# Using a streamed adaLN tile one step after its load, in a two-layer hybrid decoder trunk

## The chip, the cores and the metric

The kernel runs on one core of a Trainium2 chip. The metric is the device time of one execution in microseconds (us). Before the change the median of three runs is 1044.76 us (1042.81 to 1046.88).

The core has five engines that run side by side, each through its own list of instructions in a fixed order: TensorE (PE in the profile, its weight loads PEld), VectorE (DVE), ScalarE (ACT), GpSimd (POOL) and SyncE (SP). SyncE here only issues transfers (DMAs) between device memory and on-chip memory. An engine whose next instruction is not ready waits, and everything behind that instruction in its list waits too.

## What is computed

Two layers of a decoder trunk on 256 tokens of width 1024, in float32. In each layer a modulated LayerNorm is followed by one wide input projection, whose columns feed four token mixers (A: differential attention, B: a gated delta rule, C: latent attention, D: dilated attention over three groups), their gates z and the merge gates; then come the branch projections, an output projection and a second LayerNorm.

```python
c_act = jax.nn.silu(c)
for l in range(DEPTH):
    shift, scale, gate = jnp.split(c_act @ w_ada[l] + b_ada[l], 3, axis=-1)
    h = _layernorm(x) * (1.0 + scale[:, None, :]) + shift[:, None, :]
    y = _mixer_sublayer(h, positions, l, w_in[l], ...)
    x = _layernorm(DEEPNORM_ALPHA * x + gate[:, None, :] * y) * ln_g[l] + ln_b[l]
```

The change concerns `c_act @ w_ada[l]`, a vector of 1024 times a matrix of 1024x3072. Its result is needed at the start of a layer (shift, scale) and at its end (gate).

## The kernel before

**Weights.** Nearly all of TensorE's work multiplies the tokens by streamed weights. `load_w` loads a piece of 128x1024 floats (512 KB) into one of the `W_RAW = 4` buffers of the pool `wraw` (tile `wr`, L552); `split` (L486 to L489) then writes it as two halves: ScalarE casts the high part (`wh`, L488), VectorE subtracts it from the piece for the low part (`wl`, L489). TensorE does three matmuls for each product: `token_mm` (L598 to L600, names d, dv, m, br) and `feat_proj` (L635 to L637, names z, b). Pieces of an item are asked for `AHEAD = 2` items before the item is computed. A buffer is free again when its `wl` is written, and SyncE's queue issues the loads in a fixed order: a load whose buffer is not free holds all that stand behind it.

**The rest of adaLN.** The first modulation is loaded at the start into other buffers (L348). Everything else of it, the first layer's gate and the whole of the second layer's, is done by `ada_steps` (L360 to L370) beside the projections, in eight groups of four tiles: groups 4 and 5 of the first layer and 0 to 3 of the second during the first layer, groups 4 and 5 of the second during that layer. A tile `wada` (128x2x512, 512 KB, DMA at L364) takes a buffer of the same pool `wraw`. Its two halves are multiplied by one column of `c_act` each and added up in the tile `ada` by VectorE (`add_ada`: L312 for the first, L313 for the others). When the four tiles of a group are through, `end_ada` sums over the partitions on TensorE (`adac`, L328, or `adag`) and VectorE adds a bias (`modc`, L318, or `gateb`, L337). In the kernel before, the load and its two VectorE instructions are written in the same step.

**Streams.** `ada_steps` and the mixers are generators: each `yield` ends a step, and `step_streams` is called in the middle of a token item and after every item. A stream with rate 0.7, as ada has, gets seven steps in ten calls. So parts of the mixers are written between the matmuls of the projections: the rotary part of D's queries and keys on VectorE (`rope`, L452 to L455, into `tkd`), their transposes on TensorE (`tu_d`, L653, put off by one item through `deferred`), and the triangular inverse of B, which goes through device memory: 16 writes `scr` (L1021), four loads `g_T` and `g_U` (L1026, L1027), then products `px`, `py`, `pu`, `pw` on TensorE with copies on ScalarE (L1039, L1052) and predicated copies into `g_U` on VectorE (L1045).

**Order on each engine.** A scheduler orders each engine's list from the program and a model of durations; `in_order` adds an edge that only fixes the order of two instructions. On the chip the lists are fixed.

Of the kernel before, what the change touches and what calls it, by code (L numbers as in the profile page):

```python
# [202 lines left out]
def kernel(ctx: ExitStack, tc: tile.TileContext, d, out, dbg=None, nlayers=DEPTH):  # L203
# [18 lines left out]
    def slab(which, shape, name):  # L222
        free = int(np.prod(shape[1:]))
        assert free <= 512, (name, shape)
        t = slabs[which].tile([P, 512], F32, tag="slab", name=name)[:shape[0], 0:free]
        if len(shape) == 3:
            t = t.rearrange("p (a b) -> p a b", b=shape[2])
        elif len(shape) == 4:
            t = t.rearrange("p (a b c) -> p a b c", b=shape[2], c=shape[3])
        return t  # L230
# [40 lines left out]
    marks = {}  # L271
# [36 lines left out]
    def add_ada(acc, w, k):  # L308

        cd = cact[:, k:k + 1]  # L310
        if k == 0:
            return V.tensor_scalar(acc, w, cd, None, ALU.mult)  # L312
        return V.scalar_tensor_tensor(acc, w, cd, acc, ALU.mult, ALU.add)  # L313
# [8 lines left out]
    def end_ada(l, g, acc, tag):  # L322
        if g < 4:
            pc = bank(tag, [P, 2, 2], f"adac{l}{g}")
            terms = [(w, cact[:, k:k + 1]) for w, k in direct] + [(acc, ones[:, 0:1])]
            direct.clear()
            marks[f"sum{l}{g}"] = [
                T.matmul(pc[:, i // 2, i % 2:i % 2 + 1], a[:, i * P:(i + 1) * P], b, start=(n == 0 and i == 0),  # L328
                         stop=(n == len(terms) - 1), skip_group_check=True)
                for n, (a, b) in enumerate(terms) for i in range(4)]  # L330
            modulation(l, g, pc)
        else:
            gb = slab("b", [P, 512], f"gateb{l}{g}")
            nc.sync.dma_start(gb, d["bgate"][l:l + 1, (g - 4) * 512:(g - 3) * 512].to_broadcast([P, 512]))
            pb = bank(tag, [P, 512], f"adag{l}{g}")
            T.matmul(pb, ones, acc, start=True, stop=True)
            V.tensor_tensor(gb, pb, gb, ALU.add)  # L337
            gateb[l] = (gateb[l] or []) + [gb]
# [18 lines left out]

    first_slabs = ["p"] * 8 + ["o"] * 6 + ["c"] * 4 + ["tk"] * 4 + ["q"] * 6 + ["d"] * 4

    def ada_steps(l, g):  # L360
        acc = slab("b", [P, 512], f"ada{l}{g}")
        for kk in range(4):
            w = wraw.tile([P, 2, 512], F32, tag="wr", name=f"wada{l}{g}{kk}")
            nc.sync.dma_start(w, d["wada"][l, g, kk])  # L364
            for k in range(2):
                add_ada(acc, w[:, k, :], 2 * kk + k)
            if kk < 3:
                yield
        end_ada(l, g, acc, "sc")
        yield  # L370


    al = cpool.tile([P, DEPTH, 2], F32, name="al")
# [83 lines left out]
    def in_order(*insts):  # L457

        flat = []
        for i in insts:  # L460
            flat += i if isinstance(i, (list, tuple)) else [i]
        for a, b in zip(flat, flat[1:]):
            tc.add_manual_dep(getattr(b, "ins", b), getattr(a, "ins", a).name, mybir.DependencyInfo(mybir.DependencyClass.NoSync, mybir.DependencyReason.SCHED_ONLY),
                              reason="order of issue")
# [22 lines left out]
    def split(hi, lo, src):  # L487
        marks["hi"] = A.copy(hi, src)  # L488
        return [V.tensor_tensor(lo, src, hi.bitcast(F32), ALU.subtract)]  # L489
# [58 lines left out]
    def load_w(src, name, place=None):  # L548

        n = src.shape[-1]  # L550
        w = wraw.tile([P, 1024], F32, tag="wr", name=f"wr{name}")
        nc.sync.dma_start(w[:, 0:n], src)  # L552
        if place is None:
            width = 1024
            hi = [whp.tile([P, 1024], F32R, tag="wh", name=f"wh{name}")]
            lo = [wlp.tile([P, 1024], F32R, tag="wl", name=f"wl{name}")]
        else:
            width = n // 2
            hi = [slab(place(), [P, 512], f"wh{name}_{j}").bitcast(F32R) for j in range(2)]
            lo = [slab(place(), [P, 512], f"wl{name}_{j}").bitcast(F32R) for j in range(2)]  # L560
        marks[f"lo{name}"], marks[f"hi{name}"] = [], []
        for j, (a, b) in enumerate(zip(hi, lo)):
            m = min(n, width)
            marks[f"lo{name}"] += split(a[:, 0:m], b[:, 0:m], w[:, j * width:j * width + m])
            marks[f"hi{name}"].append(marks["hi"])

        def get(c0, m):
            return tuple(a[c0 // width][:, c0 % width:c0 % width + m] for a in (hi, lo))

        return get  # L570
# [137 lines left out]
    def layer_items(l, prev):  # L708
# [752 lines left out]
        def load_out(_):  # L1461
            place = spare()
            L.wo = [load_w(d["wout"][l, 1, p], f"o{p}_{l}", place) for p in range(4)]

        def start_ada(_):
            def steps():
                for l_, g in [(l, 4), (l, 5)] + [(l + 1, g) for g in range(4) if l + 1 < nlayers]:
                    yield from ada_steps(l_, g)
            L.sada = start("ada", steps())
# [136 lines left out]
```

## Time and profile before

| | us |
|---|---|
| median of 3 runs | 1044.76 |
| lowest, highest | 1042.81, 1046.88 |
| profiled execution | 1044.96 |
| its span | 1043.1 |
| TensorE busy | 1021.5 (98% of the span) |
| VectorE busy | 721.7 (69%) |
| ScalarE busy | 541.6 (52%) |
| DMA, share of 16 engines over the span | 53% |

The profiled execution is 1.86 us longer than its span, which is what lies around the first and the last instruction. TensorE's matmuls overlap, so the start of one to the start of the next is what one costs, and its row's duration is longer than that. The clock that was granted to TensorE is 0.992 of full speed over the span; PEclk in a window is 1.00 at full speed (2.4 GHz) and 0.50 at half (1.2 GHz). "Idle before" names the time that an engine had nothing running before an instruction, and the releaser is what ended it.

### The profile page before, as it was taken

The page shows a single profiled execution, that of the slowest core. Times are in us where ns is not written, and L with a number is a line of the kernel's source. Part 1 is how long each engine was busy: PE and PEld are TensorE (multiplying, and loading weights), DVE is VectorE, ACT ScalarE, POOL GpSimd, SP SyncE. Part 2 cuts the span into 40 slices and gives each one's busy share as a digit, 9 for nine tenths or more (in the row PEclk, how much of TensorE's full clock was granted, in tenths as well). Part 3 has the DMA queues.
Part 4 walks back from the last instruction along what each step waited for, and adds up shares of the span by engine and source line. Part 5 has one row for each costly group of instructions (what it writes and reads, how often), then busy time and mean ns, then how long its engine had stood idle before and what let it go on. Part 6 is the DMA issues. An engine that isn't in the chain of part 4 may idle for free.

```text
span 1043.1 us, 16218 instructions
## 1 busy us (share of the span) xinstructions
PE 1021.5 (98%) x5982; PEld 845.1 (81%) x5982; DVE 721.7 (69%) x1583; ACT 541.6 (52%) x1012; POOL 29.4 (3%) x38
## 2 busy tenths in 40 slices
PE   8999999999999979999999999999999999999996
PEld 4599887888887868888866988888889788888885
DVE  4788778885677646666686887788746565566676
ACT  2376675654554535555436656665445454555550
POOL 0000000010000000000000000001000000000000
PEclk8999999999999989999999999999999999999999
DMA  9964344757654576445726334465564255544541
GB/s 331 349 242 141 109 143 160 212 188 239 212 162 159 196 240 210 141 152 184 275 91 209 115 122 142 132 212 175 169 226 145 82 204 172 170 160 143 164 179 41
DMA packets 67406, 185.18 MB, mean 178 GB/s; under 512 B 13696, under 2 KB 17152, under 8 KB 67328
## 3 DMA queue, kind: packets, MB, share of 16 engines
q1 hardware_dynamic: 67328, 184.16, 53.0%
q8 instruction: 47, 0.77, 0.3%
q14 instruction: 31, 0.25, 0.1%
HBM read 179.67 MB, written 4.46 MB: 177 GB/s over the span
## 4 chain that ended last, share of the span: by engine, by line
PE 84%; DMA 8%; DVE 4%; ACT 2%; SPq 1%; issue 1%; DVEq 0%; ACTq 0%
PE m L598 6%; PE m L600 6%; PE m L599 6%; PE d L599 5%; PE d L598 5%; PE d L600 5%; DMA wada<-in_wada 4%; PE z L635 3%; PE z L637 3%; PE z L636 3%; PE br L598 3%; PE br L599 3%; PE br L600 3%; PE first L606 2%; PE b L635 2%; PE b L636 2%
## 5 line engine op out<-in xcount | busy, mean ns | idle before, releaser
L489 DVE TENSOR_TENSOR wl<-wr,wh 128x1024 fp32r<-128x1024 f32 x248 | 302.5, 1222 | 176.7 <-ACT wh L488 174.6
L488 ACT CAST wh<-wr 128x1024 fp32r<-128x1024 f32 x248 | 259.8, 1050 | 234.0 <-issue 50.2
L598 PE MATMUL m<-wh,hh 128*128 128x512 f32 x256 | 102.7, 402 | 0.0
L598 PE MATMUL d<-wh,hh 128*128 128x512 f32 x256 | 102.7, 402 | 0.0
L600 PE MATMUL d<-wh,hl 128*128 128x512 f32 x256 | 102.0, 400 | 0.0
L599 PE MATMUL d<-wl,hh 128*128 128x512 f32 x256 | 101.8, 398 | 0.0
L600 PE MATMUL m<-wh,hl 128*128 128x512 f32 x256 | 101.1, 395 | 0.0
L599 PE MATMUL m<-wl,hh 128*128 128x512 f32 x256 | 100.8, 394 | 0.0
L635 PE MATMUL z<-hh,wh 128*128 128x256 f32 x256 | 74.0, 289 | 0.0
L637 PE MATMUL z<-hh,wl 128*128 128x256 f32 x256 | 73.5, 287 | 0.0
L313 DVE SCALAR_TENSOR_TENSOR ada<-wada,cact,ada 128x512 f32<-128x512 f32 x80 | 59.7, 746 | 19.6 <-DMA wada<-in_wada 18.6
L636 PE MATMUL z<-hl,wh 128*128 128x256 f32 x256 | 73.1, 286 | 0.0
L599 PEld LDWEIGHTS d<-wl,hh 128*128 128x128 f32 x256 | 49.0, 191 | 10.6 <-issue 1.3
L600 PEld LDWEIGHTS d<-wh,hl 128*128 128x128 f32 x256 | 48.9, 191 | 10.4 <-issue 0.7
L635 PE MATMUL b<-hh,wh 128*128 128x256 f32 x192 | 56.3, 293 | 1.0 <-ACT qkva L659 1.0
L598 PEld LDWEIGHTS d<-wh,hh 128*128 128x128 f32 x256 | 49.0, 191 | 9.8 <-issue 0.5
L598 PEld LDWEIGHTS m<-wh,hh 128*128 128x128 f32 x256 | 48.1, 188 | 10.5 <-issue 0.5
L600 PEld LDWEIGHTS m<-wh,hl 128*128 128x128 f32 x256 | 48.1, 188 | 10.5 <-issue 0.5
L599 PEld LDWEIGHTS m<-wl,hh 128*128 128x128 f32 x256 | 48.2, 188 | 9.6 <-issue 0.5
L636 PE MATMUL b<-hl,wh 128*128 128x256 f32 x192 | 55.0, 286 | 0.0
L637 PE MATMUL b<-hh,wl 128*128 128x256 f32 x192 | 54.9, 286 | 0.0
L598 PE MATMUL br<-wh,bh 128*128 128x512 f32 x128 | 51.4, 401 | 0.0
(358 smaller groups left out, 2132.0 us busy)
## 6 DMA issues: line engine op xcount, KB each, us to landing
wr<-in_win SPq DMA_DIRECT2D x208, 512.0 KB
wr<-in_wbr SPq DMA_DIRECT2D x32, 512.0 KB
wada<-in_wada SPq DMA_DIRECT2D x32, 512.0 KB
wada<-in_wada SPq DMA_DIRECT2D x32, 256.0 KB
wro<-in_wout SPq DMA_DIRECT2D x8, 512.0 KB
wr<-in_wout SPq DMA_DIRECT2D x8, 512.0 KB
wrs<-in_win SPq DMA_DIRECT2D x8, 256.0 KB
wrearly<-in_win SPq DMA_DIRECT2D x8, 256.0 KB
```

The source lines that it names most:

```text
L313: return V.scalar_tensor_tensor(acc, w, cd, acc, ALU.mult, ALU.add)
L488: marks["hi"] = A.copy(hi, src)
L489: return [V.tensor_tensor(lo, src, hi.bitcast(F32), ALU.subtract)]
L598: ins.append(T.matmul(ps, a, wh, start=(first and i == 0), stop=False))
L599: ins.append(T.matmul(ps, a, wl, start=False, stop=False))
L600: ins.append(T.matmul(ps, b, wh, start=False, stop=(last and i == 1)))
L606: return [T.matmul(ps, a(2 * p + i, t), w[p](i * n, n), start=(first and i == 0), stop=(last and i == 1)) for i in range(2)]
L635: T.matmul(ps[:, f, :], wh, hh(k), start=(k == 0), stop=False)
L636: T.matmul(ps[:, f, :], wh, hl(k), start=False, stop=False)
L637: T.matmul(ps[:, f, :], wl, hh(k), start=False, stop=(k == nk - 1))
```

## The change

A list `loads` notes the last low split (`wl`) of every piece that `load_w` loads. `ada_steps` now yields right after a tile's DMA and writes the tile's two VectorE instructions in the next step of the stream; if a piece has been loaded since, the first of the two is ordered behind that piece's low split. The yield that ended a tile and the one that ended a group are gone, so a group still has four yields. DMAs, VectorE, ScalarE and TensorE instructions are the same in kind and number.

```diff
--- before.py
+++ after.py
@@ -357,17 +357,21 @@
 
     first_slabs = ["p"] * 8 + ["o"] * 6 + ["c"] * 4 + ["tk"] * 4 + ["q"] * 6 + ["d"] * 4
 
+
+    loads = []
+
     def ada_steps(l, g):
         acc = slab("b", [P, 512], f"ada{l}{g}")
         for kk in range(4):
             w = wraw.tile([P, 2, 512], F32, tag="wr", name=f"wada{l}{g}{kk}")
             nc.sync.dma_start(w, d["wada"][l, g, kk])
+            mark = len(loads)
+            yield
             for k in range(2):
-                add_ada(acc, w[:, k, :], 2 * kk + k)
-            if kk < 3:
-                yield
+                ins = add_ada(acc, w[:, k, :], 2 * kk + k)
+                if k == 0 and len(loads) > mark:
+                    in_order(loads[mark], ins)
         end_ada(l, g, acc, "sc")
-        yield
 
 
     al = cpool.tile([P, DEPTH, 2], F32, name="al")
@@ -563,6 +567,8 @@
             m = min(n, width)
             marks[f"lo{name}"] += split(a[:, 0:m], b[:, 0:m], w[:, j * width:j * width + m])
             marks[f"hi{name}"].append(marks["hi"])
+        if place is None:
+            loads.append(marks[f"lo{name}"][-1])
 
         def get(c0, m):
             return tuple(a[c0 // width][:, c0 % width:c0 % width + m] for a in (hi, lo))
```

In the changed kernel the same lines carry other numbers: L488 and L489 are L492 and L493, L452 to L455 are L456 to L459, L552 is L556, L364 is L367, L598 to L600 are L604 to L606, and the lines of B's inverse are 6 higher.

The scheduler makes a new order of all of it. The same piece has another number in the two kernels; a name's end counts tiles. First VectorE's list in the last part of the first layer, at D's third group. `wada_3969` is the first tile of the last adaLN group done in that layer, `wada_4018` the second; `d_00_4048` (before) and `d_00_4046` (after) are the same projection, and `tkd_0_4097` and `tkd_0_4095` its rotated copy, which the transposes `tu_d` on TensorE read. Before, from the piece behind `wada_3969` on:

```order
L489 TENSOR_TENSOR wl_1_3925<-wr_1_3922,wh_1_3924 128x1024
L313 SCALAR_TENSOR_TENSOR ada_3968<-wada_4018,cact,ada_3968 128x512
L489 TENSOR_TENSOR wl_2_3931<-wr_2_3928,wh_2_3930 128x1024
L452 TENSOR_TENSOR ropet_d_0_4099<-d_00_4048,ss_519 128x8x8
L313 SCALAR_TENSOR_TENSOR ada_3968<-wada_4018,cact,ada_3968 128x512
L453 TENSOR_TENSOR ropet_d_0_4099<-d_00_4048,ss_519 128x8x8
L454 TENSOR_TENSOR tkd_0_4097<-d_00_4048,cc_518 128x8x16
L489 TENSOR_TENSOR wl_3_3937<-wr_3_3934,wh_3_3936 128x1024
L452 TENSOR_TENSOR ropet_d_0_4118<-d_01_4061,ss_519 128x8x8
L453 TENSOR_TENSOR ropet_d_0_4118<-d_01_4061,ss_519 128x8x8
L454 TENSOR_TENSOR tkd_0_4116<-d_01_4061,cc_518 128x8x16
L455 TENSOR_TENSOR tkd_0_4097<-tkd_0_4097,ropet_d_0_4099 128x8x16
```

After, from the rotary work of the projection before it on:

```order
L458 TENSOR_TENSOR tkd_0_4002<-d_01_3947,cc_518 128x8x16
L313 SCALAR_TENSOR_TENSOR ada_3620<-wada_3891,cact,ada_3620 128x512
L459 TENSOR_TENSOR tkd_0_4002<-tkd_0_4002,ropet_d_0_4004 128x8x16
L456 TENSOR_TENSOR ropet_d_0_4097<-d_00_4046,ss_519 128x8x8
L457 TENSOR_TENSOR ropet_d_0_4097<-d_00_4046,ss_519 128x8x8
L458 TENSOR_TENSOR tkd_0_4095<-d_00_4046,cc_518 128x8x16
L312 TENSOR_SCALAR ada_3968<-wada_3969,cact 128x512
L459 TENSOR_TENSOR tkd_0_4095<-tkd_0_4095,ropet_d_0_4097 128x8x16
L313 SCALAR_TENSOR_TENSOR ada_3968<-wada_3969,cact,ada_3968 128x512
L493 TENSOR_TENSOR wl_1_3917<-wr_1_3914,wh_1_3916 128x1024
L318 TENSOR_TENSOR modc_3110<-adac_3962,adab 128x2x2
L493 TENSOR_TENSOR wl_2_3923<-wr_2_3920,wh_2_3922 128x1024
```

The two halves of `wada_4018` stood behind `wl_1` and inside the first projection's rotary work; they now come seven rows below the last row shown, behind the split of the first piece of the next item. The first half of `wada_3969` is not ordered behind a split here: no piece was loaded between its load and its use. The last rotary instruction of the first projection (L455, now L459) stood behind two splits, `wl_2` and `wl_3`, and now stands between the halves of `wada_3969`, ahead of `wl_1`.

Second, VectorE's list at B's inverse in the first layer. `g_U_0_2673` and `g_U_0_2677` (before) are `g_U_0_2671` and `g_U_0_2675` (after); `wada_3047` is the last tile of a group. Before:

```order
L489 TENSOR_TENSOR wl_0_2951<-wr_0_2948,wh_0_2950 128x1024
L1045 COPY_PREDICATED g_U_0_2677<-cu,py_0_2877 128x512
L313 SCALAR_TENSOR_TENSOR ada_2748<-wada_3047,cact,ada_2748 128x512 x2
L489 TENSOR_TENSOR wl_1_2957<-wr_1_2954,wh_1_2956 128x1024
L489 TENSOR_TENSOR wl_0_3061<-wr_0_3058,wh_0_3060 128x1024
L318 TENSOR_TENSOR modc_3056<-adac_3051,adab 128x2x2
L489 TENSOR_TENSOR wl_1_3067<-wr_1_3064,wh_1_3066 128x1024
L1045 COPY_PREDICATED g_U_0_2673<-cu,py_0_3035 128x512
L494 ISA prd_0_3159,mx_d_0_3161<-dsc_0_3151,cb 128x512
```

After:

```order
L493 TENSOR_TENSOR wl_0_2949<-wr_0_2946,wh_0_2948 128x1024
L313 SCALAR_TENSOR_TENSOR ada_2748<-wada_2944,cact,ada_2748 128x512
L493 TENSOR_TENSOR wl_1_2955<-wr_1_2952,wh_1_2954 128x1024
L313 SCALAR_TENSOR_TENSOR ada_2748<-wada_2944,cact,ada_2748 128x512
L493 TENSOR_TENSOR wl_0_3052<-wr_0_3049,wh_0_3051 128x1024
L313 SCALAR_TENSOR_TENSOR ada_2748<-wada_3047,cact,ada_2748 128x512
L1051 COPY_PREDICATED g_U_0_2671<-cu,py_0_3033 128x512
L1051 COPY_PREDICATED g_U_0_2675<-cu,py_0_3039 128x512
L313 SCALAR_TENSOR_TENSOR ada_2748<-wada_3047,cact,ada_2748 128x512
L493 TENSOR_TENSOR wl_1_3058<-wr_1_3055,wh_1_3057 128x1024
```

The first predicated copies no longer stand here (they are five and eight rows above the first row shown), and the last two now stand together, behind the split `wl_0_3052` and between the halves of `wada_3047`. On TensorE the products `pw`, which read both `g_U`, and `adac`, which reads `ada_2748`, now stand directly behind one another, ten matmuls into the projection z.

Third, SyncE's queue just before that inverse. Before:

```order
L552 DMA wr_0_2689<-in_win 128x1024
L552 DMA wr_1_2695<-in_win 128x1024
L552 DMA wr_2_2701<-in_win 128x1024
L552 DMA wr_3_2707<-in_win 128x1024
L1021 DMA scr<-tb_2486 8x16x16 x16
L1026 DMA g_T_0_2672<-scr 128x512
L1027 DMA g_U_0_2673<-scr 128x512
L1026 DMA g_T_0_2676<-scr 128x512
L1027 DMA g_U_0_2677<-scr 128x512
L334 DMA gateb_2684<-in_bgate 128x512
```

After:

```order
L556 DMA wr_0_2682<-in_win 128x1024
L556 DMA wr_1_2688<-in_win 128x1024
L556 DMA wr_2_2694<-in_win 128x1024
L1027 DMA scr<-tb_2484 8x16x16 x16
L1032 DMA g_T_0_2670<-scr 128x512
L1033 DMA g_U_0_2671<-scr 128x512
L1032 DMA g_T_0_2674<-scr 128x512
L1033 DMA g_U_0_2675<-scr 128x512
L556 DMA wr_3_2700<-in_win 128x1024
L334 DMA gateb_2743<-in_bgate 128x512
```

The load of the fourth piece, `wr_3`, moved from ahead of the 16 writes and four loads of B's inverse to behind them.

## Rows read from the trace of the kernel before

**Rows 1.** The page, part 1: engine, busy time, share of the span, instructions.
```profile
PE 1021.5 (98%) x5982; PEld 845.1 (81%) x5982; DVE 721.7 (69%) x1583; ACT 541.6 (52%) x1012; POOL 29.4 (3%) x38
```

**Rows 2.** Waits of TensorE: its line, what was waited for, total us, times, longest.
```profile
PE tu_d L653 <- DVE tkd L455: 5.6, 1, 5.6
...
PE pu L1051 <- DVE g_U L1045: 1.3, 1, 1.3
```

**Rows 3.** Windows: length, each engine's busy time, clock (PEclk), DMA share, GB/s.
```profile
264.00:270.00 6.00, 4.72 (x31) 4.04 (x30) 4.49 (x6) 4.29 (x6) 0.00 (x0) 1.00 0.63 212
362.00:388.00 26.00, 20.41 (x90) 16.63 (x90) 11.59 (x24) 8.62 (x15) 0.00 (x0) 0.87 0.77 261
380.00:383.70 3.70, 3.70 (x12) 3.02 (x11) 0.73 (x1) 1.59 (x3) 0.00 (x0) 0.50 0.97 397
```

**Rows 4.** Timeline of TensorE, 373 to 384: start, duration, instruction, [idle before <- releaser].
```profile
373.45 0.39 PE L599 MATMUL d<-wl,hh 128*128 128x512 f32 x1
373.67 0.39 PE L600 MATMUL d<-wh,hl 128*128 128x512 f32 x1
379.65 1.09 PE L653 MATMUL tu_d<-cf,tkd 128*128 128x128 f32 x4 [5.59 <-DVE tkd L455]
380.38 0.78 PE L598 MATMUL d<-wh,hh 128*128 128x512 f32 x1
...
383.52 0.50 PE L599 MATMUL d<-wl,hh 128*128 128x512 f32 x1
383.85 0.40 PE L600 MATMUL d<-wh,hl 128*128 128x512 f32 x1
```

**Rows 5.** Timeline of VectorE, 338 to 380.
```profile
342.36 0.75 DVE L313 SCALAR_TENSOR_TENSOR ada<-wada,cact,ada 128x512 f32<-128x512 f32 x1 [0.47 <-DMA wada<-in_wada]
...
362.51 1.23 DVE L489 TENSOR_TENSOR wl<-wr,wh 128x1024 fp32r<-128x1024 f32 x1
...
369.84 0.49 DVE L312 TENSOR_SCALAR ada<-wada,cact 128x512 f32<-128x512 f32 x1 [5.32 <-DMA wada<-in_wada]
...
374.70 0.75 DVE L313 SCALAR_TENSOR_TENSOR ada<-wada,cact,ada 128x512 f32<-128x512 f32 x1 [2.44 <-DMA wada<-in_wada]
...
377.63 1.21 DVE L489 TENSOR_TENSOR wl<-wr,wh 128x1024 fp32r<-128x1024 f32 x1
...
379.22 0.48 DVE L455 TENSOR_TENSOR tkd<-tkd,ropet_d 128x128 f32<-128x128 f32 x2
```

**Rows 6.** Timeline of SyncE's queue, 338 to 372.
```profile
338.85 0.33 SPq L364 DMA_DIRECT2D wada<-in_wada  x1
...
363.76 0.33 SPq L364 DMA_DIRECT2D wada<-in_wada  x1
...
371.14 0.33 SPq L364 DMA_DIRECT2D wada<-in_wada  x1
```

**Rows 7.** Waits of VectorE, the same columns as for TensorE.
```profile
DVE ada L313 <- DMA wada<-in_wada: 18.6, 16, 3.6
```

**Rows 8.** Timeline of VectorE, 249 to 267, at B's inverse.
```profile
249.90 0.69 DVE L337 TENSOR_TENSOR gateb<-adag,gateb 128x512 f32<-128x512 f32 x1 [5.92 <-DMA gateb<-in_bgate]
...
265.48 1.23 DVE L489 TENSOR_TENSOR wl<-wr,wh 128x1024 fp32r<-128x1024 f32 x1 [2.79 <-ACT wh L488]
266.62 0.72 DVE L1045 COPY_PREDICATED g_U<-cu,py 128x512 f32<-128x512 uint8 x1
```

**Rows 9.** Timeline of ScalarE, 264 to 266.
```profile
264.40 1.05 ACT L488 CAST wh<-wr 128x1024 fp32r<-128x1024 f32 x1 [5.66 <-DMA wr<-in_win]
```

**Rows 10.** Timeline of SyncE's queue, 243 to 244.
```profile
243.18 0.32 SPq L1027 DMA_DIRECT2D g_U<-scr  x1
```

**Rows 11.** Timeline of SyncE's queue, 753, in the second layer.
```profile
753.30 11.62 SPq L552 DMA_DIRECT2D wr<-in_win  x6
```

**Rows 12.** Timeline of VectorE, 761, in the second layer.
```profile
761.91 1.23 DVE L489 TENSOR_TENSOR wl<-wr,wh 128x1024 fp32r<-128x1024 f32 x1 [1.75 <-ACT wh L488]
```

**Rows 13.** Timeline of TensorE, 252.
```profile
252.16 0.39 PE L599 MATMUL dv<-wl,hh 128*128 128x512 f32 x1
```

## The prediction

> **What bounds the kernel now.** I read the page's busy times first: TensorE is busy 1021.5 us, 98% of the span [rows 1]. So the change can gain at most what TensorE still waits for, and it loses whatever new wait it gives TensorE. Next the waits of TensorE, sorted by length: one stands out, the transposes `tu_d`, which waited once, 5.59 us, for VectorE's last rotary instruction; the next of the kind that the change touches is `pu`, which waited 1.28 us once for a predicated copy [rows 2]. Then windows around the long wait: in 362 to 388 us TensorE worked 20.41 of 26 us at a mean clock of 0.87, and in 380 to 383.7 it was granted 0.50 of full speed, 1.2 GHz instead of 2.4 [rows 3]. Then the timelines of the engines there, to follow the wait back.
>
> TensorE started its last matmul before the gap at 373.67 and the transposes at 379.65 [rows 4]. What they waited for ended on VectorE behind 379.22 [rows 5]. That instruction had its inputs long before; it stood behind the splits of three pieces and these behind adaLN tiles. VectorE's row at 369.84 says "5.32 us, a DMA of wada", the one at 374.70 "2.44, a DMA of wada" [rows 5]. Both tiles were asked for late: the first at 363.76, right when the split begun at 362.51 set a buffer free, the second at 371.14, right when VectorE was through with the first [rows 5, 6]. So it is a ring: VectorE stands at an adaLN tile that is still on its way, the splits queue behind it, no buffer comes free, and so the next adaLN tile is asked for only once VectorE is through with the last one. With nothing in its way a tile takes 3.51 us from its issue to its first use (338.85 to 342.36), the second tile here 3.56, the first 6.08, since three other loads were issued right behind it [rows 5, 6]. VectorE waited 18.6 us in 16 such places for the later halves alone [rows 7], but only this one reached TensorE.
>
> **The change, part by part.** Nothing is added or removed on any engine: 64 VectorE instructions move, with them the order of their neighbours, and a few DMAs in SyncE's queue. So the sum is made of waits only, against the profiled execution, 1044.96 us, which lies 0.20 above the median of the runs.
>
> *The ring at 363 to 380.* In the new list the rotary instruction that TensorE waits for stands directly behind the first half of `wada_3969` and ahead of all three splits, and both halves of `wada_4018` stand behind the next item's first piece. One wait for a tile is left ahead of it. That tile's buffer is now freed by the second half of `wada_3891`, two VectorE instructions of 0.75 us [rows 5] later than before at most, so I put its issue at 363.76 + 1.5 = 365.3 and its use, after the same 6.08, at 371.3; the half takes 0.49 and the rotary instruction about 0.3 (the row of 379.22 has two in 0.48 [rows 5]), so 372.1. TensorE wants it at its last matmul's start and one pitch, 373.67 + 0.23 = 373.9 [rows 4]. It is in time by 1.8 us, so the wait goes: **−5.59**. The three splits behind it end at about 372.8 + 3 x 1.2 = 376.4 and are wanted one after the other from about 376 on, when `tu_d` and six matmuls are through; each is ready by then.
>
> *The clock.* Eight matmuls from 380.38 to 383.85 took 3.47 us, where the pitch at full speed is 0.22 (373.45 to 373.67), so 8 x 0.22 = 1.8 would do: 1.6 lost [rows 4]. The four transposes took 379.65 to 380.38, 0.73 us, at half speed, so 0.37 too much [rows 4]. With the gap gone the clock has no reason in this trace to fall: **−2.0**.
>
> [...]
>
> *B's inverse in the first layer.* The wait of 1.28 us: a predicated copy at 266.62 stood behind a split at 265.48 that waited for a cast, which itself had waited 5.66 us for its piece [rows 8, 9]. In the new list the first two predicated copies stand higher, ahead of that split, so this wait goes: −1.28. But the last two now stand behind `wl_0_3052`, and `pw` and `adac` on TensorE, in one block, behind them. No row shows that wait. It is 0 if the piece is in time. At most it is the 5.66 us that ScalarE stood before the cast in the old place. The nearest row is the old wait itself, the same instruction behind the same kind of split: **−1.28 + 1.28 = 0**.
>
> *The moved load.* `wr_3` is now asked for behind the writes and loads of the inverse, after 243.18 + 0.36 = 243.5 [rows 10]. In the second layer the old list already has this order, and there a piece asked for at 753.30 had its split begun at 761.91, 8.6 us later, plus 1.23 for the split [rows 11, 12]. By that row the split here ends at 253.4, and TensorE wants the piece's low part at about 252.16, where it first used it [rows 13]: 1.2 us late. By the layer's own row it is earlier: VectorE was held until 249.90 by the gate bias, whose instruction now stands ahead of this split [rows 8]; 249.90 + 0.69 + 1.22 = 251.8, in time. I take the nearer row, this layer's: **0**, and keep 1.2 for the range.
>
> *All other places.* Buffers are held one step longer by each of the 32 tiles, and SyncE's queue stands at a load whose buffer isn't free. What hides that is that pieces are mostly split well ahead of TensorE. VectorE's other waits for adaLN tiles get shorter or go, but TensorE did not wait there: 0. Below nothing it can be worth up to 1 us, the small waits of `py` and its like.
>
> The sum: 1044.96 − 5.59 − 2.0 + 0 + 0 = 1037.4. With the best ends (no new wait, and 1 us of small ones gone) it is 1035.1; with the worst of the two unknown places (5.66 − 1.28 and 1.2 more) it is 1043.0.
>
> **The rivals.**
>
> *The stall moves to the inverse.* One of the two new places stalls TensorE as long as the old one did: 5.66 us, with the slow clock's 2.0 behind it. For it speaks that there ScalarE already stood 5.66 us at a load [rows 9] and that two copies, a half tile and `adac` now share one split. Against it: the copies waited only 1.28 before. Time: 1037.4 + 5.66 + 2.0 − 1.28 = 1043.8, no change that can be told.
>
> *The ring is not opened.* The first use of `wada_3969` is not ordered behind a split in the new list, since no piece is loaded in between, and from the buffer's release to it stand only rotary instructions, 0.7 us of work where a load takes 3.5 to 6.1 [rows 5, 6]. If that load comes 1.8 us later than I put it, TensorE waits again for the rest; half the old wait with the slow clock is 2.8 + 2.0, less what it takes away: 1037.4 + 4.8 = 1042.2.
>
> *The four buffers become the bound (slower).* A tile that stays a step longer leaves three buffers for the pieces; loads then start later than TensorE needs them, and it waits for low parts at the tightest places, B's inverse in both layers. It decides once a piece is more than its lead late, 1 to 3 us there. With a stall as long as the old one and its slow clock at both, 7.6 each, the time is 1037.4 + 2 x 7.6 = 1052.6. For it speaks the window 380 to 383.7, where the DMA engines are 0.97 busy [rows 3], and that a wait on a load can hold an engine for 5.66 us [rows 9]; against it that most pieces have a lead.
>
> The Trainium skill ("Perfetto Trace Analysis", section "Optimization Strategy") holds that a gap that repeats on the engine which should be full can mean too few buffers for the next tile. The trace before shows two single waits and none that repeats [rows 2]; by the rule the slower rival would show as a row of equal gaps.
>
> **How the numbers follow.** The forecast has a chance of 0.56, the moved stall 0.22, the ring not opened 0.12, the slower case 0.10. About 0.5%, 5.2 us, is what a measurement of this kernel can tell from no change. The forecast's own range, 1035 to 1040, lies nearly all below 1039.5 and gives 0.52 to faster and 0.04 to the same; the two middle rivals give 0.03 to faster, 0.29 to the same and 0.02 to slower, since runs differ by 4 us; the last gives 0.08 to slower and 0.02 to the same. So faster 0.55, same 0.35, slower 0.10. The range runs from 1034.5, the best end less half a us, to 1045, which holds both middle rivals; the slower case stays outside.
>
> **What would show it.** Right: no wait of `tu_d` for VectorE at 370 to 380 us, clock 1.00 in all windows from 370 to 390, both waits for `wada` of that stretch gone but for one of up to some 5 us at the first tile, and the waits of `pu` replaced by one at `pw` or `adac` of about 1 us near 272. Wrong: a gap of several us on TensorE at 250 to 275 or 760 to 770, PEclk of 0.5 outside the start and the end of the span, or gaps that wait for `wl` one after the other.

## The result, and the profile after

The changed kernel takes 1039.82 us, median of 5 runs (1038.33 to 1041.38), against 1044.76 (1042.81 to 1046.88, 5 runs): ratio 0.9950, 95% interval 0.9935 to 0.9965. That is 4.9 us less, where 7.4 had been forecast against the same median. The interval leaves out 1, so these runs show a gain, though it is no more than the 5.2 us that the prediction took as the least that can be told from no change. The profiled execution is the slowest of the five, 1041.38 with a span of 1039.6, so the two profiles differ by 3.6 only.

The page's first part and the waits of TensorE after, which answer to [rows 1, 2]:

```profile
PE 1021.8 (98%) x5982; PEld 844.9 (81%) x5982; DVE 721.1 (69%) x1583; ACT 541.9 (52%) x1012; POOL 33.1 (3%) x38
```

```profile
PE tu_d L659 <- DVE tkd L459: 3.2, 1, 3.2
...
PE br L604 <- ACT mg L1423: 0.8, 1, 0.8
```

The wait of `pu` is gone. The wait of `tu_d` is 3.2 us in place of 5.6, but it is another one. Windows of both kernels show where TensorE stood; the second number is the window's length, the third TensorE's busy time, and the clock stands behind the five engines. First before:

```profile
240.00:280.00 40.00, 38.69 (x230) 33.28 (x229) 24.22 (x40) 19.35 (x31) 0.00 (x0) 1.00 0.74 247
360.00:400.00 40.00, 34.41 (x158) 28.36 (x157) 21.35 (x41) 15.76 (x26) 0.00 (x0) 0.91 0.73 248
480.00:520.00 40.00, 40.00 (x184) 33.07 (x183) 27.31 (x36) 20.59 (x30) 0.00 (x0) 1.00 0.76 254
720.00:800.00 80.00, 78.99 (x454) 67.03 (x452) 50.41 (x95) 40.58 (x67) 4.51 (x2) 1.00 0.56 180
```

After:

```profile
240.00:280.00 40.00, 40.00 (x240) 35.07 (x238) 22.85 (x35) 18.57 (x28) 0.00 (x0) 1.00 0.79 257
360.00:400.00 40.00, 36.76 (x171) 30.20 (x171) 23.92 (x45) 17.93 (x29) 0.00 (x0) 0.96 0.79 264
480.00:520.00 40.00, 39.21 (x181) 31.96 (x180) 25.59 (x34) 19.21 (x30) 0.00 (x0) 1.00 0.72 244
720.00:800.00 80.00, 80.00 (x478) 69.02 (x477) 51.55 (x100) 42.56 (x69) 5.21 (x2) 1.00 0.60 190
```

At B's inverse no idle time is left, where it was 1.31 us in the first layer (240 to 280) and 1.01 in the second (720 to 800). In 360 to 400 there are 3.24 in place of 5.59, and 480 to 520 has 0.79 that were not there.

Idle time is not yet time gained. A firmer measure is a point up to which TensorE has done the same matmuls in both kernels, counted by their kind in the two traces: the difference between its two times is what has been gained by then. The row `dpo` is such a point, with 2077 matmuls ahead of it; first before, then after:

```profile
354.86 1.09 PE L1390 MATMUL dpo<-PT,dvv 128*64 128x128 f32 x16
```

```profile
355.04 1.09 PE L1396 MATMUL dpo<-PT,dvv 128*64 128x128 f32 x16
```

So here, past B's inverse, the changed kernel is 0.18 us behind, although it stood 1.31 us less: its matmuls between 175 and 355 us took that much longer from start to start, `dsc` 0.6 and `br` 0.5 us, and several other kinds a little. At three later points it is ahead: by 2.42 behind D's third group (a row of `z`, 463.19 for 465.61), by 1.25 where the second layer begins (`first`, 534.56 for 535.81) and by 3.43 behind the second layer's inverse (`m`, 840.86 for 844.29).

The timeline of VectorE after, which answers to [rows 5]:

```profile
371.76 0.49 DVE L312 TENSOR_SCALAR ada<-wada,cact 128x512 f32<-128x512 f32 x1 [3.16 <-DMA wada<-in_wada]
372.17 0.28 DVE L459 TENSOR_TENSOR tkd<-tkd,ropet_d 128x128 f32<-128x128 f32 x1
...
382.78 1.54 DVE L313 SCALAR_TENSOR_TENSOR ada<-wada,cact,ada 128x512 f32<-128x512 f32 x2
...
386.18 1.23 DVE L493 TENSOR_TENSOR wl<-wr,wh 128x1024 fp32r<-128x1024 f32 x1 [0.71 <-ACT wh L492]
...
387.79 1.21 DVE L493 TENSOR_TENSOR wl<-wr,wh 128x1024 fp32r<-128x1024 f32 x1
388.92 0.28 DVE L459 TENSOR_TENSOR tkd<-tkd,ropet_d 128x128 f32<-128x128 f32 x1
```

The first half of `wada_3969` waited 3.16 us and the rotary instruction behind it came at 372.17, in time. The ring is open: both halves of `wada_4018` ran at 382.78 without a wait. But at 388.92 the same instruction of D's next projection stands behind two splits (386.18 and 387.79), and TensorE waits for it. TensorE after, which answers to [rows 4]:

```profile
374.08 0.60 PE L659 MATMUL tu_d<-cf,tkd 128*128 128x128 f32 x4
...
380.92 0.60 PE L659 MATMUL tu_d<-cf,tkd 128*128 128x128 f32 x4
...
385.72 0.39 PE L606 MATMUL d<-wh,hl 128*128 128x512 f32 x1
389.35 0.63 PE L659 MATMUL tu_d<-cf,tkd 128*128 128x128 f32 x4 [3.24 <-DVE tkd L459]
389.73 0.64 PE L604 MATMUL d<-wh,hh 128*128 128x512 f32 x1
...
393.15 0.47 PE L606 MATMUL d<-wh,hl 128*128 128x512 f32 x1
```

The transposes that had waited 5.59 us before are those of 374.08; they and the next ones, of 380.92, waited for nothing, and those of 389.35, of the next projection, waited 3.24. Eight matmuls then took 389.73 to 393.15, 3.42 us, where 8 x 0.22 = 1.8 do: 1.7 lost to half clock once more.

### The profile page after: what moved, and what is told of

Same layout as the page of the kernel before. It is cut to its first block, busy times and chain, and to the rows that moved or that the text cites. A ratio compares the mean times of both kernels' runs of the same rounds, so it can differ in the third digit from the quotient of the medians.

```text
span 1039.6 us, 16220 instructions
## 1 busy us (share of the span) xinstructions
PE 1021.8 (98%) x5982; PEld 844.9 (81%) x5982; DVE 721.1 (69%) x1583; ACT 541.9 (52%) x1012; POOL 33.1 (3%) x38
## 4 chain that ended last, share of the span: by engine, by line
PE 86%; DMA 7%; DVE 3%; ACT 2%; issue 1%; SPq 1%; DVEq 0%; ACTq 0%
PE m L604 5%; PE m L606 5%; PE m L605 5%; PE d L605 5%; PE d L606 5%; PE d L604 5%; PE z L641 3%; PE z L642 3%; PE z L643 3%; DMA wada<-in_wada 3%; PE br L604 3%; PE br L606 3%; PE br L605 3%; PE first L612 2%; PE b L641 2%; PE b L642 2%
## 5 line engine op out<-in xcount | busy, mean ns | idle before, releaser
L493 DVE TENSOR_TENSOR wl<-wr,wh 128x1024 fp32r<-128x1024 f32 x248 | 302.5, 1222 | 184.1 <-ACT wh L492 181.5
L492 ACT CAST wh<-wr 128x1024 fp32r<-128x1024 f32 x248 | 259.8, 1050 | 225.4 <-DMA wr<-in_win 45.3
L604 PE MATMUL m<-wh,hh 128*128 128x512 f32 x256 | 102.7, 402 | 0.0
L606 PE MATMUL d<-wh,hl 128*128 128x512 f32 x256 | 102.0, 399 | 0.0
L604 PE MATMUL d<-wh,hh 128*128 128x512 f32 x256 | 101.7, 399 | 0.0
L606 PE MATMUL m<-wh,hl 128*128 128x512 f32 x256 | 101.0, 395 | 0.0
L606 PEld LDWEIGHTS d<-wh,hl 128*128 128x128 f32 x256 | 48.9, 191 | 10.1 <-issue 0.7
L604 PEld LDWEIGHTS d<-wh,hh 128*128 128x128 f32 x256 | 48.9, 191 | 9.7 <-issue 0.2
L604 PEld LDWEIGHTS m<-wh,hh 128*128 128x128 f32 x256 | 48.1, 188 | 10.5 <-issue 0.5
L606 PEld LDWEIGHTS m<-wh,hl 128*128 128x128 f32 x256 | 48.1, 188 | 10.5 <-issue 0.8
L604 PE MATMUL br<-wh,bh 128*128 128x512 f32 x128 | 52.1, 407 | 0.8 <-ACT mg L1423 0.8
```

Source lines behind the costliest of these rows:

```text
L604: ins.append(T.matmul(ps, a, wh, start=(first and i == 0), stop=False))
L606: ins.append(T.matmul(ps, b, wh, start=False, stop=(last and i == 1)))
```

## The experiments

Ratios are to the kernel before on the same chip (median 1046.09 us for the first four, 1045.67 for the fifth to eighth, 1045.74 for the last two), with 95% intervals; they are taken over all runs and need not be the quotient of the two medians. `late` in a diff stands for the new form of `ada_steps` (yield, then the two instructions with the edge), which is the old one where `late` is false.

**The wait that is left (first and second).** The first adds two order edges to the changed kernel:

```diff
+FIRST = {'d1110_0': '30_2'}
...
+        cp = A.copy(tk[:, :, 16:64], pv[:, :, 16:64])
+        last = rope(tk[:, :, 0:16], pv[:, :, 0:16], 8, 8, name, t)
+        if name in FIRST:
+            in_order(cp, marks[f"hi{FIRST[name]}"])
+            in_order(last, marks[f"lo{FIRST[name]}"])
```

> The changed kernel with two order edges more: the copy and the last rotary instruction of one rotated tile (D's projection d12, first token half, first layer) stand ahead of the cast and the low split of the next item's third piece. Nothing else moves but some rows around it. In the changed kernel the transposes tu_d wait 3.24 us for that rotary instruction at 386 to 389 us, and the clock is 0.5 for some 3.5 us behind it, about 1.9 us lost. Theory 'order': the wait is there only because the rotary instruction stands behind the splits of two pieces that TensorE does not need yet; with the edges no wait takes its place, no half clock, 1039.8 - 3.2 - 1.9 = 1034.7. Theory 'late pieces': the pieces come so late, because 2 MB of x and of the second LayerNorm's weights are loaded in the same stretch, that TensorE waits for the low parts wl instead: at least half of the wait comes back, 1038 to 1040.

Measured: 1037.82, ratio 0.9922 (0.9905 to 0.9938). Its waits of TensorE:

```profile
PE dsc L1369 <- DVE modc L319: 0.9, 1, 0.9
...
PE tu_d L663 <- DVE tkd L460: 0.3, 1, 0.3
```

Of 3.24 us 0.31 are left, the clock is 1.00 through 376 to 400, and 0.9 come at `dsc` a little later. In this stretch the wait was one of order: the two pieces whose splits stood ahead were not needed yet, and no wait for a low part took its place. The span is 3.3 us shorter than the changed kernel's, not 5; these two rows are 1.2 of the rest, and about half a us is not accounted for. The median, 1037.82, misses both theories: 'order' had 1034.7, 'late pieces' 1038 or more.

The second moves other loads out of the stretch:

```diff
-            nc.sync.dma_start(tiles[u], src[:, u])
+            ins = nc.sync.dma_start(tiles[u], src[:, u])
+            if "dma" in marks:
+                in_order(marks["dma"], ins)
...
-                    nc.sync.dma_start(lnw[i][b], d[nm][l:l + 1, ...])
+                    in_order(marks["dma"], nc.sync.dma_start(lnw[i][b], d[nm][l:l + 1, ...]))
```

Here `marks["dma"]` is the last piece's load written so far.

> The changed kernel with the reload of x (4 x 256 KB) and the loads of the second LayerNorm's weights (4 x 256 KB) ordered behind pieces of a later item, so that they leave the stretch 363 to 390 us. The order on VectorE moves too, by 16 rows: the rotary instruction of 386 us comes to stand ahead of two more splits. Both theories, 'order' and 'late pieces': the wait of tu_d at 386 us and its half clock go, about 1034.7. What tells them apart is in the trace: 'late pieces' expects the load that is issued near 377 us and takes 7.7 us in the changed kernel to take about 3.5 to 4.5, and the first adaLN tile's wait of 3.16 us on VectorE to fall below 1; 'order' alone would leave these as they are. A rival: x and the weights now come late at the end of the layer (480 to 500 us), and TensorE waits there: 1037 or more.

Measured: 1036.22 (1035.01 to 1036.64), ratio 0.9907 (0.9892 to 0.9922): the fastest version here, with the eighth. `tu_d` waits for nothing at 360 to 400. Twelve us from the second adaLN tile's load on, in the changed kernel and then in this one:

```profile
373.00:385.00 12.00, 12.00 (x58) 9.92 (x57) 7.67 (x13) 4.70 (x8) 0.00 (x0) 1.00 0.88 308
```

```profile
371.00:383.00 12.00, 12.00 (x60) 9.95 (x59) 8.35 (x16) 5.89 (x12) 0.00 (x0) 1.00 0.75 225
```

The DMA engines are 0.75 busy in place of 0.88. In the changed kernel the next item's third piece is issued at 377.29 and cast at 385.10, 7.8 us later; the rows are those of the second and the third piece:

```profile
383.17 1.05 ACT L492 CAST wh<-wr 128x1024 fp32r<-128x1024 f32 x1 [1.56 <-DMA wr<-in_win]
...
385.10 1.05 ACT L492 CAST wh<-wr 128x1024 fp32r<-128x1024 f32 x1 [0.34 <-DMA wr<-in_win]
```

In the second experiment the third piece is issued at 374.78 and cast at 382.97, and its cast waits for nothing; the second piece's, at 381.09, waits for a buffer that TensorE reads, and only the first piece's still waits for its load:

```profile
376.95 1.05 ACT L494 CAST wh<-wr 128x1024 fp32r<-128x1024 f32 x1 [2.67 <-DMA wr<-in_win]
...
381.09 1.05 ACT L494 CAST wh<-wr 128x1024 fp32r<-128x1024 f32 x1 [0.88 <-PE d L608]
...
382.97 1.06 ACT L494 CAST wh<-wr 128x1024 fp32r<-128x1024 f32 x1
```

The first adaLN tile's wait on VectorE fell from 3.16 to 1.51, not below 1. So loads do come earlier without these 2 MB. The rival, a new wait at 480 to 500, did not show: two waits of `br` there and later are 0.8 us together. The order moved too, to one in which the rotary instruction stands ahead of these splits, so whether earlier pieces alone would remove the wait of 3.24 stays open; the first experiment shows that the order alone does.

**Which part of the change opens the ring (third, fourth, tenth).** Three kernels have the new form in some groups only. The condition of the third is shown; in the fourth it is `!= (1, 3)`, in the tenth `== (1, 2)`:

```diff
+            late = (l, g) == (1, 3)
+            if late:
+                yield
```

> The kernel before, with the change in one of the eight adaLN groups only, the last one of the first layer (the tiles of 363 to 395 us). The lists differ from the ones before only in that stretch (8 rows replaced on VectorE). Theory 'ring': the whole gain is made here, since the second tile no longer holds VectorE: the wait of 5.59 us shrinks to 1 to 2 us (the first tile is still waited for and three splits still stand ahead of the rotary instruction) and its half clock goes; then the wait of 3.24 us with its half clock follows at 386 as in the changed kernel: about 1044.8 - 4 - 2 + 5.1 = 1044. Theory 'elsewhere': what the change gains comes from B's inverse in both layers (1.3 + 1.0 us of waits) and from earlier splits ahead of the stretch, and then this kernel is as before, 1044 to 1045, with the 5.59 us in place or merely moved.

Measured: 1041.41, ratio 0.9953 (0.9935 to 0.9970). TensorE's waits in 370 to 396:

```profile
376.08 0.63 PE L665 MATMUL tu_d<-cf,tkd 128*128 128x128 f32 x4 [1.34 <-DVE tkd L465]
...
389.24 0.63 PE L665 MATMUL tu_d<-cf,tkd 128*128 128x128 f32 x4 [1.10 <-DVE tkd L465]
```

The wait of 5.59 became 1.34, as expected from a second tile that no longer holds VectorE, and the one at 389 is 1.10 and not 3.24; no half clock in either. It gains more than either theory said.

> The complement: the changed kernel, with the old form in the last adaLN group of the first layer alone. Its lists differ from the changed kernel's only in rows of 363 to 395 us. Theory 'ring': with the old form in that group the ring is back, the wait of about 5 us with its half clock too, and what is left is the gain at B's inverse in both layers, 1.3 + 1.0: about 1042.5. Theory 'elsewhere': the order ahead of the stretch already puts the rotary instruction ahead of the splits, so that the old form does no harm there: about 1039 to 1040, as the changed kernel.

Measured: 1038.20, ratio 0.9931 (0.9915 to 0.9948), and one wait there:

```profile
387.78 0.63 PE L665 MATMUL tu_d<-cf,tkd 128*128 128x128 f32 x4 [1.34 <-DVE tkd L465]
```

Theory 'ring' in that form falls. With the last group used at once, and so with the old hold on its second tile, no wait is left at 374 to 380, since the rotary instruction already stands ahead of the splits. What put it there is the delay of the group before. The next projection's wait is 1.34 in place of 3.24, at full speed: there the rotary instruction stands behind the third piece and no longer behind the fourth as well.

> The kernel before, with the change in the group before the last one of the first layer only (its tiles come at 320 to 365 us). At B's inverse the order is the old one; at 363 to 390 us the rotary instruction stands ahead of the splits as in the changed kernel, though the last group's tiles are used as early as before. Theory 'two places': the wait of 5.59 us and its half clock go, about 1.3 us of wait comes at 388 us, and the old wait at B's inverse stays, with its half clock in some runs: ratio 0.993 to 0.996, with a wide spread. Theory 'ring': what opens it is the use of the last group's own second tile behind later splits, so this kernel keeps a wait of 3 us or more: ratio 0.998 or above.

Measured: 1040.36, ratio 0.9938 (0.9916 to 0.9961). The new form in that one group gives as much as the whole change, as far as the intervals tell, with B's inverse in the old order; the row of `adac` is its wait there:

```profile
PE adac L328 <- DVE ada L313: 1.5, 1, 1.5
...
PE tu_d L665 <- DVE tkd L465: 1.2, 1, 1.2
```

Theory 'ring' falls here too: VectorE's rotary instruction ran at 371.26, ahead of the splits, and the transposes behind it did not wait.

**The inverse alone (ninth).** `late = (l, g) in ((0, 4), (0, 5), (1, 0))`.

> The kernel before, with the change in the first three adaLN groups only. VectorE's list is then the changed kernel's up to and through B's inverse in the first layer, and the old one from there on, at 363 to 390 us too. Theory 'two places': the wait at B's inverse (1.28 us in the profile of the kernel before, 1.9 and 2.0 us with a half clock of 3.6 and some 13 us behind it in two other kernels with the same order there) goes whole, no wait at pw or adac comes in its place; the 5.6 us of tu_d and its half clock stay. Ratio to before 0.996 to 0.998, and the times spread less than the 8 to 10 us of the kernels with the old order. Theory 'ring alone': the gain is all in 363 to 390 us, ratio 0.999 or above; or a new wait of about 1.3 us at pw or adac, as the prediction took it.

Measured: 1045.48 (1042.98 to 1050.81), ratio 0.9998 (0.9983 to 1.0014).

```profile
240.00:280.00 40.00, 40.00 (x233) 34.66 (x232) 22.90 (x32) 18.85 (x29) 0.00 (x0) 1.00 0.77 247
360.00:400.00 40.00, 34.89 (x158) 28.78 (x157) 22.12 (x42) 16.72 (x27) 0.00 (x0) 0.91 0.76 249
```

The wait at the inverse is gone and none came in its place, yet no gain can be seen, and the spread is not smaller. Theory 'two places' fails as to the time: 1.3 us lie inside this interval, but 2.6 or more do not. 'Ring alone' had this ratio, and the trace says why. The row `dpo`, behind the same 2077 matmuls, starts at 357.23, 2.37 us later than in the kernel before. Of these 1.67 were there at 34 us already (the granted clock of the first 40 us is 0.87 in this profile and 0.91 in that of the kernel before). The other 0.7 came on the way through the inverse, although a wait of 1.28 is gone there: rows that show no wait took 2.0 longer. Two more waits came near the ends of the layers:

```profile
PE br L610 <- ACT mg L1429: 1.7, 2, 1.0
```

So a wait that goes in one row can be paid in others; here and in the changed kernel the first layer's inverse gave no time.

**Order and contention in the kernel before (fifth and sixth).** The fifth adds edges of the first experiment's kind to the kernel before, ahead of the second piece's cast and split and of the second adaLN tile; the sixth moves the loads as the second does.

> The kernel before, adaLN as it was, with order edges alone: the copy and the last rotary instruction of the tile that tu_d waits 5.59 us for (D's projection d11, first token half, first layer) stand ahead of the cast and split of the next item's second piece and ahead of the second adaLN tile of the group. The adaLN tiles are used as early as before. Theory 'order': the wait is lost time only because the rotary instruction stands behind splits; the 5.59 us and the half clock go, and what is left is a wait of at most 1.3 us for the low parts wl at 376 to 380 us, since the second tile still holds VectorE to 374.7: ratio to before about 0.994 (6 us less). Theory 'ring': VectorE standing at the second tile delays the three splits behind it all the same, TensorE waits for wl instead of tkd, 3 us or more: ratio 0.997 or above.

Measured: 1043.61 (1041.53 to 1050.73), ratio 0.9993 (0.9974 to 1.0012).

```profile
378.41 0.50 PE L600 MATMUL d<-wl,hh 128*128 128x512 f32 x1 [0.30 <-DVE wl L490]
...
391.81 0.63 PE L658 MATMUL tu_d<-cf,tkd 128*128 128x128 f32 x4 [3.32 <-ACT wh L489]
```

At 374 to 380 the wait fell to 0.30, as 'order' has it; then the next projection's transposes waited 3.32. The profile names a cast, but the transposes do not read its output. They read the tile of a rotary instruction that ended 0.14 us ahead of them, where the changed kernel has 0.15 (389.20 and 389.35):

```profile
391.39 0.28 DVE L456 TENSOR_TENSOR tkd<-tkd,ropet_d 128x128 f32<-128x128 f32 x1
```

So this is most likely the same wait for VectorE once more: its list has splits, both halves of an adaLN tile and another split ahead of that instruction. The queue shows one reason why these come late:

```profile
378.38 1.06 SPq L553 DMA_DIRECT2D wr<-in_win  x2
```

The next item's first piece was asked for only when a split behind the second adaLN tile freed a buffer; before, it was asked for at 373.95. Neither theory had that: the held tile's delay comes out one projection, some 13 us, later. The profiled execution has a span of 1040.3, 2.8 less than before; over all runs that is not borne out.

> The kernel before, with the reload of x and the loads of the second LayerNorm's weights moved out of 363 to 390 us; VectorE's list is as before but for 3 rows. Theory 'contention': these 2 MB make the two adaLN tiles late (6.08 and 3.56 us from issue to use); without them the first takes about 3.5 to 4.5, the second too, the wait of 5.59 shrinks to 3 or less: ratio 0.996 to 0.998. Theory 'order': VectorE still stands at both tiles and the rotary instruction still behind three splits, so a wait of 3 us or more remains, with the half clock. Against both: the wait is gone altogether.

Measured: 1044.56 (1040.78 to 1049.10), ratio 0.9993 (0.9973 to 1.0012). VectorE's first wait for a tile (the second is 1.83, at 375.90), and TensorE's wait:

```profile
371.01 0.49 DVE L314 TENSOR_SCALAR ada<-wada,cact 128x512 f32<-128x512 f32 x1 [3.90 <-DMA wada<-in_wada]
```

```profile
380.85 1.09 PE L655 MATMUL tu_d<-cf,tkd 128*128 128x128 f32 x4 [4.33 <-DVE tkd L457]
```

The first tile takes 4.66 us from its issue at 366.35, where it took 6.08, and TensorE's wait is 4.33 for 5.59, with the clock at 0.50 behind it: about 1.3 us of the wait go with the 2 MB. This is what 'order' had; that the rest is order is shown by the fourth and tenth, where it goes with the order alone. Moving the loads gains nothing that can be told here.

**The edge (seventh).** The changed kernel without its two lines `if k == 0 and len(loads) > mark: in_order(loads[mark], ins)`.

> The changed kernel without the order edge: each tile is used one step after its load, but its first use isn't ordered behind a split. VectorE's list at 363 to 390 us then has the rotary instruction behind three splits and the second tile between the first two, as before. Theory 'the edge makes the order': a wait of 4 to 6 us of tu_d with half clock at 370 to 384 as before, and only the gains at B's inverse remain: ratio 0.998. Theory 'a step later is enough': as the changed kernel, 0.995.

Measured: 1050.56 (1047.15 to 1058.56), ratio 1.0053 (1.0033 to 1.0073): slower. In its profile `tu_d` waits 4.87 us with a half clock behind, and B's inverse stalls as well:

```profile
273.96 2.78 PE L1041 MATMUL px<-g_U,g_LL 128*128 128x128 f32 x16 [1.99 <-ACT g_T L1056]
277.48 1.87 PE L328 MATMUL adac<-ones,ada 128*128 128x1 f32 x8 [0.74 <-DVE ada L313]
```

```profile
276.00:278.00 2.00, 1.26 (x7) 0.96 (x6) 1.40 (x3) 1.09 (x2) 0.00 (x0) 0.50 0.82 197
280.00:284.00 4.00, 4.00 (x11) 2.70 (x10) 1.30 (x2) 2.83 (x5) 0.00 (x0) 0.50 0.93 328
284.00:288.00 4.00, 4.00 (x18) 3.73 (x18) 2.74 (x6) 0.81 (x2) 0.00 (x0) 0.50 0.38 92
288.00:292.00 4.00, 4.00 (x28) 3.70 (x29) 2.35 (x6) 0.82 (x2) 0.00 (x0) 0.91 0.22 90
```

The clock was 0.50 from about 276 to 288. In this kernel the delay by a step alone is a loss; with the order edge it is a gain. The wait of `tu_d` is what 'the edge makes the order' expected; the loss beyond the kernel before was expected by neither theory. The profiled execution (1058.56) is the slowest of twelve, 8 us above the median, so it is not shown that the stall at the inverse makes the loss at the median.

**Both (eighth).** The second experiment with the fourth's condition.

> The version with x and the LayerNorm's weights loaded later (1036.2, ratio 0.991), with the last adaLN group of the first layer in the old form, which in the changed kernel cost nothing (0.993 against 0.995). If the old form there is better in itself (the tile's buffer is freed earlier), this is 0.990 or below; if it only happened to avoid the second wait of 3.24 us, which the later loads have removed already, it is as that version, 0.991.

Measured: 1036.44, ratio 0.9911 (0.9890 to 0.9932), no different from the second. The last group's new form costs nothing once the loads are out of the way.

## Why the prediction was right or wrong

**The ring: right.** The first tile was issued at 366.29 (forecast 365.3), used at 371.76 (371.3), and the rotary instruction ended at 372.45 (372.1); `tu_d` did not wait, 5.59 gone. Its size was right, its cause was half right: the fourth and tenth experiments show that the delay of the group before puts the rotary instruction ahead of the splits. The late use of the last group's own tiles, which the prediction gave equal weight, opens the ring too when it is done alone (third).

**The clock: right for that stretch.** 1.00 in place of 0.50 there, 2.0 gone.

**What is late next: wrong.** This is the step that failed. The prediction followed the rotary instruction and the three splits behind it, found them in time, and put everything further on under "all other places", at nothing. It did not ask when the next projection's rotary instruction would come. In the changed order it stands behind the third and, for its last part, the fourth piece of the next item:

```
L493 TENSOR_TENSOR wl_2_4035<-wr_2_4032,wh_2_4034 128x1024
L456 TENSOR_TENSOR ropet_d_0_4193<-d_00_4142,ss_519 128x8x8
L457 TENSOR_TENSOR ropet_d_0_4193<-d_00_4142,ss_519 128x8x8
L458 TENSOR_TENSOR tkd_0_4191<-d_00_4142,cc_518 128x8x16
L493 TENSOR_TENSOR wl_3_4041<-wr_3_4038,wh_3_4040 128x1024
L459 TENSOR_TENSOR tkd_0_4191<-tkd_0_4191,ropet_d_0_4193 128x8x16
```

The old list has the third piece ahead of it too, but not the fourth. Before, TensorE's transposes ran there at 393.46 without a wait, and the casts waited for TensorE, not for loads. Now TensorE was there at 386.1, 7.3 us earlier, about as forecast, and the third piece's cast had waited for its load to 385.10. 3.24 us and 1.7 of half clock came back: two thirds of what the ring had cost. It is the first rival, the moved stall, at another place than the one named and at 4.9 in place of 7.7.

**B's inverse in the first layer: the sum right, its terms wrong.** The old wait of 1.28 went; the new one, put at 1.28, was 0. `pw` started at 274.49, when the first copy behind `wl_0_3052` was through and the second nearly. Yet the net was about 0 as forecast (0.18 us behind at `dpo`), because matmuls around it took as much longer without a row that waits. That the 0 came out is luck: no term of the prediction stands for this loss, and no run shows what causes it.

**The moved load: right**, 0: no gap in 240 to 280. **All other places:** put at 0, with 1 us as the "best end". From 535 to 844 us, past the second layer's inverse, 2.2 us were gained, of which rows of waits show 1.0. Between 466 and 536, 1.2 us were lost, 0.79 of them at `br`, which waits for a gate `mg` on ScalarE.

The sum by the points of equal work, at the times of the kernel before: +0.2 up to 355 us, −2.6 from there to 466, +1.2 to 536 and −2.2 to 844, together −3.4, against −3.6 between the two profiled executions and −4.9 between the medians. The −2.6 is what the terms of the ring give: −5.59 − 2.0 + 3.24 + 1.7 = −2.65. What is left of the 4.9 stays open; executions of one kernel differ by that much.

That the time lay well within the range is partly luck: 4.9 us came back at the next projection and 1.2 were lost between 466 and 536, which the forecast did not have, and the second layer gave 2.2 that it did not have either. Together that is the 4.0 by which the profiled execution lies above 1037.4.

**The slower rival** (four buffers) did not come: no row of equal gaps. A held buffer can be seen once: in the changed kernel `wada_4018` keeps its buffer from its load's issue at 373.14 to the end of its use at 384.3, and the next item's fourth piece was asked for at 382.89 only. In the first experiment the tile is held as long (372.92 to 384.05), and with the rotary work ahead TensorE waits 0.31 us there.

## What to carry to other kernels

Where a wait goes, let the engine that waited arrive earlier at everything behind it, and check the next instruction of the same kind for the same queue in front of it: here the same line stalled again one projection later. A late use of a loaded tile paid here only with an order edge that says behind what it is to stand; without it the scheduler put the tile back in front of the splits and the kernel was slower. Bulk loads that are not urgent (here 2 MB for the layer's end) are worth moving out of a stretch in which pieces are only just in time, but not by themselves: in the changed kernel, where the order moved too, that went with a further gain (0.9907 for 0.9950), in the kernel before with none (0.9993). And idle time that goes from a profile is to be checked against the start of a later row behind the same work: 1.3 us of it here was no time at all.

## What the runs showed of the hardware that was not expected

How long TensorE stands does not by itself say whether its clock falls. It stayed at full speed behind gaps of 1.28 (kernel before), 1.34 (third experiment), 2.33 (third, at 61.79) and 3.32 us (fifth, at 391.81), and fell to half behind 1.51 (tenth, at 268.03: 0.64 in 268 to 272), 1.90 (fifth, at 269.24), 1.99 (seventh, at 273.96), 3.24, 4.33, 4.87, 5.11 and 5.59. The two windows behind the fifth's gaps, the short one first:

```profile
270.00:272.00 2.00, 2.00 (x9) 1.64 (x9) 1.53 (x3) 1.53 (x3) 0.00 (x0) 0.70 0.87 225
272.00:274.00 2.00, 2.00 (x6) 1.56 (x5) 0.00 (x0) 0.15 (x1) 0.00 (x0) 0.50 1.02 385
392.00:396.00 4.00, 4.00 (x20) 3.38 (x19) 3.06 (x7) 0.84 (x3) 0.00 (x0) 1.00 0.90 303
396.00:400.00 4.00, 4.00 (x25) 3.46 (x24) 0.00 (x0) 1.00 (x1) 0.00 (x0) 1.00 0.50 168
```

The Trainium skill ("TensorE: Matmul & The Clock Gate", section "HAM oscillation — how this bites in real kernels") describes a kernel in which TensorE waits some 3 to 5 us for data ahead of each burst and starts every burst at the slow clock. Here the gaps of 3.24, 4.33 and 4.87 us agree with that and the one of 3.32 does not; the shorter gaps that were followed by half speed are not what that section describes. So the price of a half clock is best kept as a range: 0 or the 2.0 us that it cost before, and once 6 (the seventh experiment's 12 us at half speed, behind two small gaps).

The clock also makes much of the difference between executions of one kernel. Of the ninth experiment's twelve, the quickest took 1042.98 us at a mean granted clock of 0.995 and the slowest 1050.81 at 0.987; what is missing to full clock, (1 − clock) times the time, is 5.2 us in the first and 13.7 in the second, and that is all of the 7.8 between them. Part of it lies at the start: the first 40 us have 0.91 in the profiles of the kernel before and the changed one, 0.96 in the second, third and tenth, 0.87 in the sixth and ninth, 0.83 in the seventh. So two single profiles can differ by some us in a stretch that the edit was not made for.
